# GpSimd makes more of the low weight parts in layer 1's mixer projections

## The chip, the cores and the metric

One core of a Trainium2 chip runs the whole kernel in one launch. The metric is the device time of one execution in microseconds. Five engines work from queues of their own, each strictly in the order in which the program puts instructions into it: TensorE (PE, with its weight loads as PEld), VectorE (DVE), ScalarE (ACT), GpSimd (POOL) and SyncE (SP), which here only starts transfers.

## The reference, cut to what matters

A two-layer decoder over 272 positions (16 meta tokens and 256 of the sequence), width 2048, float32. Each layer is a mixer and then a gated convolution FFN, with a residual around each. The change is in layer 1's mixer, whose first step is one large projection:

```
def mixer_cd(h, w_in, ...):
    z = h @ w_in                                  # 272 x 2048 by 2048 x 6416
    z_gla, z_rw = z[..., :GLA_COLS], z[..., GLA_COLS:]
    q, k, v, go, glr = jnp.split(z_gla, _splits(GLA_SIZES), axis=-1)
    ...
    o = gla_chunked(q, k, v, log_a)               # chunked gated linear attention
    ...
    r, kr, vr, xw, xa, xg = jnp.split(zr, _splits(RW_SIZES), axis=-1)
    ...
    y = rwkv7_scan(r, decay, kr, vr, kk, a)       # a recurrence over positions
    ...
    return jnp.concatenate([o, y], axis=-1) @ w_out
```

The kernel does the recurrence `rwkv7_scan` in chunks of 64 positions, for which it needs inverses of small triangular matrices: 128 of 32x32 and 16 of 16x16.

## The kernel before

Everything is a chain of weight multiplications of one form. A weight of 2048 rows by 128 columns is one projection; the mixer of layer 1 has 50 of them, called by `proj` in the order of the packed tensor `cd_in`. `gemm` and `gemm_steps` work a projection through in four parts of 512 columns of the packed weight (`SUB` = 4 tiles of 128x128). For precision each float32 weight part is split in two: ACT casts `wf` to a high part `wh` (L161), and another engine subtracts it again and leaves the low part `wl` (L163). Then PE runs three matmuls for each of the four tiles: high weight by high activation (L181), high by low (L182), low by high (L183). So a projection is 4 casts, 4 subtractions and 48 matmuls; its first matmul on the third low part is the 27th of them.

Who subtracts is decided by the argument `pool_lo`: the parts whose number (0 to 3) is in it go to GpSimd, the rest to VectorE:

```
eng = G if (k0 + s0) // SUB in pool_lo else V
lo = eng.tensor_sub(wl[:, :ns * P], src, wh[:, :ns * P].bitcast(F32))
```

`wh` and `wl` have five buffers each, so a part can be made at most five parts, one and a quarter projections, ahead of the matmuls that use it. Layer 0's mixer gives parts 0, 1 and 2 to GpSimd in most of its projections; layer 1's mixer gives it none.

The 50 projections of layer 1's mixer come in three blocks. The first ten (numbers 24, 25 and 8 to 15 of the recurrence's columns) bring the ranks, the gate and the keys. The next 24 are those of the gated linear attention, six for each of four heads; beside them runs the generator `prep`, which builds the recurrence's matrices (`stage_a`, `stage_b`, `stage_c` for eight head pairs) and inverts them. The last 16 bring the recurrence's `r` and `v`, and `rw_scan` runs beside them and beside the output projection.

The inversion is `lanes` (L645 to L665). It is GpSimd work from end to end: it fetches the matrices with a DMA issued on GpSimd's queue (L647), makes an identity (L649, L650), and does forward substitution, 31 steps of one multiplication (L656) and one addition (L658), each on the result of the step before, for the 32x32 matrices; the same with 15 steps for the 16x16 ones; a copy (L661); and DMAs to DRAM and back in another order (L662, L664, then L764, L767, L769), some of which wait on GpSimd's queue until an earlier one has landed. In the kernel before GpSimd has nothing else in its queue from the first step on until these are through.

The order in each engine's queue is not the order of the source: a scheduler in the framework sets it when the program is built, from its own estimate of durations, and it is fixed from then on.

Of the kernel before, what the change touches and what calls it, by code (L numbers as in the profile page):

```python
# [21 lines left out]
T = NM + SEQ  # L22
# [73 lines left out]
def _body(ctx, tc, nc, A):  # L96
# [47 lines left out]
    def tick():  # L144
        for t in list(side):
            try:
                next(t)
            except StopIteration:
                side.remove(t)
# [36 lines left out]
    def gemm(w, g, xs, n, pool_lo=()):  # L186
        acc = psA.tile([P, T], F32, tag="acc", name="acc")
        for _ in gemm_steps(w, g, xs, len(xs), acc[:, :n], pool_lo):
            tick()
        return acc[:, :n]  # L190
# [305 lines left out]
    def mixer_cd(tp, nm):  # L496
        xs = nm.xs()
        gi = [0]

        def proj(c0=0):  # L500
            gi[0] += 1
            return gemm(A["cd_in"], gi[0] - 1, [(a[:, c0:], b[:, c0:]) for a, b in xs], T - c0)

        def ring(name):
            return hpool.tile([P, T], F32, tag="h", name=name)
# [1 line left out]
        def shift(dst, i, c0=0, ps=None):  # L507
            if ps is None:
                ps = proj(c0)
            z = tp.tile([P, T + 16], F32, tag="z", name="z", bufs=2)  # L510
            V.tensor_mul(z[:, 1 + c0:T + 1], ps, nm.rstd[:, c0:])
            if c0:
                c0 += 1
                V.memset(dst[:, 0:c0], 0.0)
            else:
                V.memset(z[:, 0:1], 0.0)
            t = tp.tile([P, T], F32, tag="zt", name="zt", bufs=2)
            S.activation(t[:, c0:], z[:, 1 + c0:T + 1], AF.Copy, scale=omm[:, i:i + 1])
            V.scalar_tensor_tensor(dst[:, c0:], z[:, c0:T], pc("mu", i), t[:, c0:], op0=ALU.mult, op1=ALU.add)
# [22 lines left out]

        xt = ring("xt")
        ps24 = proj()
        nm.finish()
        glr = ring("glr")
        V.tensor_mul(glr, acc, nm.rstd)
        shift(xt, 24, 0, ps24)
        ps25 = proj(OUT - 2)
        logs, LD = [], []  # L550
        for q in range(4):
# [497 lines left out]
        c0, n = OUT, T - OUT  # L1049
# [146 lines left out]
```

## Time and profile before

| | |
|---|---|
| median of 3 runs | 2456.9 us (2455.43 to 2460.22) |
| the profiled execution | 2460.71 us, of which its span, first to last instruction, is 2458.9 us |
| PE busy | 2429.6 us, 99% of the span |
| DVE busy | 1792.7 us, 73% |
| ACT busy | 1338.1 us, 54% |
| POOL busy | 570.8 us, 23% |
| granted TensorE clock, mean | 0.998 |

Busy time counts an engine's instructions and not its waits, so a share is only an average over stages; which engine is late in a stage is read from that stage's windows and waits. Layer 1's mixer, up to its last scan, lies between about 1130 and 1640 us of the span.

### The profile page before, as it was taken

The page shows a single profiled execution, that of the slowest core. Times are in us where ns is not written, and L with a number is a line of the kernel's source. Part 1 is how long each engine was busy: PE and PEld are TensorE (multiplying, and loading weights), DVE is VectorE, ACT ScalarE, POOL GpSimd, SP SyncE. Part 2 cuts the span into 40 slices and gives each one's busy share as a digit, 9 for nine tenths or more (in the row PEclk, how much of TensorE's full clock was granted, in tenths as well). Part 3 has the DMA queues.
Part 4 walks back from the last instruction along what each step waited for, and adds up shares of the span by engine and source line. Part 5 has one row for each costly group of instructions (what it writes and reads, how often), then busy time and mean ns, then how long its engine had stood idle before and what let it go on. Part 6 is the DMA issues. An engine that isn't in the chain of part 4 may idle for free.

```text
span 2458.9 us, 53575 instructions
## 1 busy us (share of the span) xinstructions
PE 2429.6 (99%) x20476; PEld 2372.9 (97%) x20476; DVE 1792.7 (73%) x3400; ACT 1338.1 (54%) x2573; POOL 570.8 (23%) x894
## 2 busy tenths in 40 slices
PE   8999999999999999999999999999999999999998
PEld 8999999999999999999999988899999999999998
DVE  8897797777556677667786678879777755777754
ACT  5444655555445555546745445545656544656653
POOL 5677240000000000121148044416101000101122
PEclk9999999999999999999999999999999999999999
DMA  6555555555565555666445332345555566555564
GB/s 220 189 177 180 169 174 176 180 180 175 177 181 182 177 178 178 185 194 189 148 146 176 127 129 82 101 132 178 189 188 183 183 196 195 187 183 188 178 196 151
DMA packets 130991, 423.95 MB, mean 172 GB/s; under 512 B 18832, under 2 KB 27088, under 8 KB 130736
## 3 DMA queue, kind: packets, MB, share of 16 engines
q1 hardware_dynamic: 129104, 417.34, 53.0%
q8 instruction: 161, 2.64, 0.4%
q0 software_dynamic: 912, 2.55, 0.4%
q14 instruction: 94, 0.77, 0.1%
q10 hardware_dynamic: 720, 0.66, 0.1%
HBM read 414.41 MB, written 5.93 MB: 171 GB/s over the span
## 4 chain that ended last, share of the span: by engine, by line
PE 95%; DVE 2%; ACT 1%; DMA 1%; POOL 1%; issue 1%; SPq 0%; DVEq 0%; ACTq 0%; POOLq 0%
PE acc L181 24%; PE acc L183 23%; PE acc L182 23%; PE acc L176 7%; PE acc L175 7%; PE acc L174 6%; PE ps L932 1%; PE ps L966 1%; PE ps L947 0%; PE acc L178 0%; PE ps L981 0%; PE ps L834 0%; PE ps L989 0%; DVE wl L163 0%; DMA wf<-ab_in 0%
## 5 line engine op out<-in xcount | busy, mean ns | idle before, releaser
L161 ACT CAST wh<-wf 128x512 fp32r<-128x512 f32 (+1 forms) x1576 | 955.9, 611 | 876.8 <-PE acc L182 600.8
L163 DVE TENSOR_TENSOR wl<-wf,wh 128x512 fp32r<-128x512 f32 (+1 forms) x1465 | 1027.9, 707 | 463.7 <-ACT wh L161 418.8
L181 PE MATMUL acc<-x,wh 128*128 128x272 f32 (+2 forms) x2438 | 710.5, 291 | 1.3 <-ACT wh L161 1.3
L183 PE MATMUL acc<-x,wl 128*128 128x272 f32 (+2 forms) x2438 | 699.3, 287 | 1.0 <-DVE wl L163 1.0
L182 PE MATMUL acc<-x,wh 128*128 128x272 f32 (+2 forms) x2438 | 698.6, 287 | 0.0
L181 PEld LDWEIGHTS acc<-x,wh 128*128 128x128 f32 x2438 | 458.8, 188 | 15.4 <-issue 7.5
L183 PEld LDWEIGHTS acc<-x,wl 128*128 128x128 f32 x2438 | 458.9, 188 | 3.3 <-DVE wl L163 1.9
L182 PEld LDWEIGHTS acc<-x,wh 128*128 128x128 f32 x2438 | 459.6, 189 | 1.1 <-issue 0.3
L182 PE MATMUL acc<-act,wh 128*128 128x272 f32 (+1 forms) x1408 | 396.0, 281 | 0.0
L183 PE MATMUL acc<-act,wl 128*128 128x272 f32 (+1 forms) x1408 | 396.0, 281 | 0.0
L181 PE MATMUL acc<-act,wh 128*128 128x272 f32 (+1 forms) x1408 | 396.0, 281 | 0.0
L174 PE MATMUL acc<-x,wh 128*128 128x260 f32 x1144 | 323.6, 283 | 0.0
L176 PE MATMUL acc<-x,wl 128*128 128x258 f32 x1144 | 321.8, 281 | 0.0
L175 PE MATMUL acc<-x,wh 128*128 128x256 f32 x1144 | 321.0, 281 | 0.0
L181 PEld LDWEIGHTS acc<-act,wh 128*128 128x128 f32 x1408 | 264.8, 188 | 0.0
L182 PEld LDWEIGHTS acc<-act,wh 128*128 128x128 f32 x1408 | 264.7, 188 | 0.0
L183 PEld LDWEIGHTS acc<-act,wl 128*128 128x128 f32 x1408 | 264.7, 188 | 0.0
L175 PEld LDWEIGHTS acc<-x,wh 128*128 128x128 f32 x1144 | 215.6, 188 | 0.0
L174 PEld LDWEIGHTS acc<-x,wh 128*128 128x128 f32 x1144 | 215.5, 188 | 0.0
L176 PEld LDWEIGHTS acc<-x,wl 128*128 128x128 f32 x1144 | 215.3, 188 | 0.0
L163 POOL TENSOR_TENSOR wl<-wf,wh 128x512 fp32r<-128x512 f32 x111 | 148.1, 1342 | 57.3 <-ACT wh L161 54.9
L459 POOL MEMSET u<- 128x2 f32 x88 | 8.6, 100 | 573.3 <-DVE c L272 566.4
(341 smaller groups left out, 3743.9 us busy)
## 6 DMA issues: line engine op xcount, KB each, us to landing
wf<-up SPq DMA_DIRECT2D x352, 512.0 KB, 3.5
wf<-down SPq DMA_DIRECT2D x128, 512.0 KB, 3.8
wf<-cd_in SPq DMA_DIRECT2D x100, 512.0 KB, 3.6
wf<-ab_in SPq DMA_DIRECT2D x76, 512.0 KB, 3.6
wf<-down SPq DMA_DIRECT2D x64, 384.0 KB, 3.2
wf<-ab_out_s SPq DMA_DIRECT2D x16, 512.0 KB, 3.8
wf<-ab_out_a SPq DMA_DIRECT2D x16, 512.0 KB, 3.6
wf<-cd_out_o SPq DMA_DIRECT2D x16, 512.0 KB, 3.6
```

Source lines behind the costliest of these rows:

```text
L161: last_hi[0] = S.copy(wh[:, :ns * P], src)
L163: lo = eng.tensor_sub(wl[:, :ns * P], src, wh[:, :ns * P].bitcast(F32))
L174: PE.matmul(acc, a, x4, start=kk == 0, stop=False)
L175: PE.matmul(acc[:, 4:], a, x0, start=False, stop=False)
L176: PE.matmul(acc[:, 2:], b, x2, start=False, stop=False)
L181: PE.matmul(acc, a, xh, start=kk == 0, stop=False)
L182: PE.matmul(acc, a, xl, start=False, stop=False)
L183: PE.matmul(acc, b, xh, start=False, stop=kk == kt - 1)
L459: G.memset(u[:, 0:2], 0.0)
L932: PE.matmul(gv[:, :128], bkc, t[r, h0], start=True, stop=True)
L966: PE.matmul(wy[H[h0], 0:64], t[:, h0, 0:64], sv[:, h0], start=True, stop=True)
```

## The change

`proj` hands `gemm` a set of parts for GpSimd. In the first ten projections it is parts 1 and 3, so two of four; in the 40 after them it is part 2, one of four. That makes 20 + 40 = 60 subtractions of 128x512, moved from VectorE's queue to GpSimd's. Nothing is added or left out.

```diff
         def proj(c0=0):
             gi[0] += 1
-            return gemm(A["cd_in"], gi[0] - 1, [(a[:, c0:], b[:, c0:]) for a, b in xs], T - c0)
+            return gemm(A["cd_in"], gi[0] - 1, [(a[:, c0:], b[:, c0:]) for a, b in xs], T - c0,
+                        (1, 3) if gi[0] <= 10 else (2,))
```

The statement takes one line more than before, so every line below it has a number higher by one in the changed kernel: L656, L658 are L657, L659 there.

The scheduler places the moved subtractions in GpSimd's queue. In the orders below `wl` is a low part, `lanes` and `tm` are the inversion's matrix and its product. First the inversion of the 32x32 matrices, around its ninth and tenth step, before:

```order
L656 TENSOR_TENSOR tm<-lanes 128x192
L658 TENSOR_TENSOR lanes<-lanes,tm 128x24x8
L656 TENSOR_TENSOR tm<-lanes 128x207
L658 TENSOR_TENSOR lanes<-lanes,tm 128x23x9
L656 TENSOR_TENSOR tm<-lanes 128x220
L658 TENSOR_TENSOR lanes<-lanes,tm 128x22x10
```

The same queue now, at the three places in the inversion where a low part stands (rows between them are steps of the inversion alone):

```order
L659 TENSOR_TENSOR lanes<-lanes,tm 128x24x8
L657 TENSOR_TENSOR tm<-lanes 128x207
L163 TENSOR_TENSOR wl<-wf,wh 128x512
L659 TENSOR_TENSOR lanes<-lanes,tm 128x23x9
...
L659 TENSOR_TENSOR lanes<-lanes,tm 128x14x18
L163 TENSOR_TENSOR wl<-wf,wh 128x512
L657 TENSOR_TENSOR tm<-lanes 128x247
...
L657 TENSOR_TENSOR tm<-lanes 128x60
L163 TENSOR_TENSOR wl<-wf,wh 128x512
L659 TENSOR_TENSOR lanes<-lanes,tm 128x2x30
```

These are the third low parts of projections 20, 21 and 22, counted along PE's queue from the mixer's first. The one of projection 19 stands ahead of the first step, behind the DMA that fetches the matrices. Between that step and the part of projection 20 there are 17 multiplications and additions, then 19 up to the part of projection 21, then 23 up to the part of projection 22.

The second place is the end of the inversion, where GpSimd's queue holds DMAs. Before:

```order
L664 DMA scrN<-lanes 128x1024
L662 DMA scrT<-lanes 128x1024
L656 TENSOR_TENSOR tm<-lane_17689,lane_17688 16x28
L658 TENSOR_TENSOR lane_17689<-lane_17689,tm 16x14x2
L656 TENSOR_TENSOR tm<-lane_17689,lane_17688 16x39
L764 DMA tn<-scrN 32x32x32
L658 TENSOR_TENSOR lane_17689<-lane_17689,tm 16x13x3
L767 DMA lt<-scrT 32x32x32
```

Now:

```order
L657 TENSOR_TENSOR tm<-lane_17689,lane_17688 16x39
L765 DMA tn<-scrN 32x32x32
L163 TENSOR_TENSOR wl<-wf,wh 128x512
L659 TENSOR_TENSOR lane_17689<-lane_17689,tm 16x13x3
L768 DMA lt<-scrT 32x32x32
L657 TENSOR_TENSOR tm<-lane_17689,lane_17688 16x48
L768 DMA lt<-scrT 32x32x32
L659 TENSOR_TENSOR lane_17689<-lane_17689,tm 16x12x4
L765 DMA tn<-scrN 32x32x32
L163 TENSOR_TENSOR wl<-wf,wh 128x512
```

Here the low parts of projections 23 and 24 stand among the transfers that bring the inverses back; those of 25, 26 and 27 follow behind the rest of the transfers, behind the 16x16 steps and behind the last transfer. PE's own order of matmuls in these projections, the side work between them included, is the same before and now.

## Rows read from the trace of the kernel before

**Rows 1.** The page: busy time, share and instructions of each engine.
```profile
PE 2429.6 (99%) x20476; PEld 2372.9 (97%) x20476; DVE 1792.7 (73%) x3400; ACT 1338.1 (54%) x2573; POOL 570.8 (23%) x894
```

**Rows 2.** Windows of two stretches: length, busy PE, PEld, DVE, ACT, POOL, clock, DMA.
```profile
1280.00:1360.00 80.00, 80.00 (x615) 75.21 (x614) 55.53 (x95) 42.42 (x80) 62.07 (x104) 1.00 0.56 169
1420.00:1640.00 220.00, 218.04 (x2132) 184.28 (x2131) 182.48 (x509) 112.33 (x363) 84.29 (x173) 1.00 0.33 105
```

**Rows 3.** Waits of PE, 1130 to 1690: us in total, times, longest.
```profile
PE ps L728 <- DVE bk L716: 1.2, 2, 1.1
PE ps L932 <- POOL arc L922: 1.0, 2, 0.9
PE acc L183 <- DVE wl L163: 1.0, 3, 0.4
```

**Rows 4.** The page's groups of the subtraction: busy us, mean ns of one, idle before.
```profile
L163 DVE TENSOR_TENSOR wl<-wf,wh 128x512 fp32r<-128x512 f32 (+1 forms) x1465 | 1027.9, 707 | 463.7 <-ACT wh L161 418.8
...
L163 POOL TENSOR_TENSOR wl<-wf,wh 128x512 fp32r<-128x512 f32 x111 | 148.1, 1342 | 57.3 <-ACT wh L161 54.9
```

**Rows 5.** Timeline of POOL in the inversion: start us, us, instruction, idle before.
```profile
1276.05 0.51 POOL L647 DMA_DIRECT2D lane<-scr  x1
...
1276.60 0.31 POOL L649 MEMSET lane<- 16x256 f32 x1
...
1279.47 0.23 POOL L656 TENSOR_TENSOR tm<-lanes 128x31 f32<-128x31 f32 x1 [2.38 <-DMA lanes<-scr]
...
1291.54 1.08 POOL L658 TENSOR_TENSOR lanes<-lanes,tm 128x207 f32<-128x207 f32 x1
...
1308.67 0.60 POOL L656 TENSOR_TENSOR tm<-lanes 128x247 f32<-128x247 f32 x1
...
1325.27 0.36 POOL L658 TENSOR_TENSOR lanes<-lanes,tm 128x60 f32<-128x60 f32 x1
...
1337.24 0.80 POOL L767 DMA_DIRECT2D lt<-scrT  x1 [3.44 <-DMA scrT<-lanes]
...
1356.11 1.08 POOL L769 DMA_DIRECT2D lt<-scr0T  x2 [4.12 <-DMA scr0T<-lane]
```

**Rows 6.** Timeline of ACT: the cast for the third part of projection 19.
```profile
1278.82 0.62 ACT L161 CAST wh<-wf 128x512 fp32r<-128x512 f32 x1 [0.52 <-PE acc L182]
```

**Rows 7.** Timeline of PE: first matmul on the third low part, projections 20, 21, 22, 27.
```profile
1290.98 0.29 PE L183 MATMUL acc<-x,wl 128*128 128x272 f32 x1
...
1298.34 0.28 PE L183 MATMUL acc<-x,wl 128*128 128x258 f32 x1
...
1307.06 0.28 PE L183 MATMUL acc<-x,wl 128*128 128x258 f32 x1
...
1342.73 0.28 PE L183 MATMUL acc<-x,wl 128*128 128x258 f32 x1
```

**Rows 8.** Lines L656 and L658, 1291.6 to 1308.6: duration ns min/median/max.
```profile
L656 POOL TENSOR_TENSOR tm<-lanes x9: 566/622/961, 1292.7 to 1306.9; 128x252 f32<-128x252 f32 x2, 128x255 f32<-128x255 f32 x2, 128x220 f32<-128x220 f32 x1, 128x231 f32<-128x231 f32 x1
L658 POOL TENSOR_TENSOR lanes<-lanes,tm x10: 687/985/1214, 1291.5 to 1307.6; 128x252 f32<-128x252 f32 x2, 128x255 f32<-128x255 f32 x2, 128x207 f32<-128x207 f32 x1, 128x220 f32<-128x220 f32 x1
```

**Rows 9.** Timeline of PE at the start of the kernel: start us, us.
```profile
7.42 0.59 PE L181 MATMUL ps<-x,wh 128*128 128x272 f32 x1 [7.42 <-ACT wh L161]
...
13.10 0.43 PE L182 MATMUL ps<-x,wh 128*128 128x272 f32 x1
13.32 0.35 PE L183 MATMUL ps<-x,wl 128*128 128x272 f32 x1
```

**Rows 10.** Windows, the stretch after the last matmul: columns as in Rows 2.
```profile
2450.00:2455.00 5.00, 0.00 (x0) 0.00 (x0) 3.48 (x11) 0.00 (x0) 3.25 (x5) 0.56 0.80 281
```

**Rows 11.** Timeline of PE: first matmul on the fourth low part of projection 4.
```profile
1162.43 0.39 PE L183 MATMUL acc<-x,wl 128*128 128x272 f32 x1 [0.21 <-DVE wl L163]
```

**Rows 12.** Timelines in layer 0's mixer: subtractions of POOL and DVE that meet.
```profile
64.92 1.29 POOL L163 TENSOR_TENSOR wl<-wf,wh 128x512 fp32r<-128x512 f32 x1
...
65.01 1.75 DVE L163 TENSOR_TENSOR wl<-wf,wh 128x512 fp32r<-128x512 f32 x1
```

## The prediction

> **What bounds the kernel now.** I read the page's busy times first: PE is busy for 2429.6 of 2458.9 us [rows 1], so the kernel is one queue of matmuls, and an edit counts only by what it does to PE's waits. Next the windows of layer 1's mixer: PE 80.00 of 80 us in the stretch of the inversion, 218.04 of 220 in that of the scan, while DVE has 55.53 and 182.48 [rows 2]. So DVE, from which the change takes work, leaves PE little to wait for. PE's own waits in the mixer say the same: for DVE they come to 1.2 and 1.0 us, for POOL to 1.0 [rows 3]. The 2.2 us are about all that a quicker DVE can give back. Third I read GpSimd's timeline, since it gets the work: it is idle for most of the mixer, but in the inversion it is busy for 62.07 of 80 us [rows 2], in a row of steps that wait for each other. PE has no use for the inverses until much later, so that chain costs nothing today. It begins at 1279.47 and its last transfer is issued by 1357.19 (1356.11 + 1.08) [rows 5].
>
> **The change, part by part.** Moved are 60 subtractions. DVE loses 60 x 0.707 = 42 us of work; GpSimd gets 60 x 1.342 = 81 us [rows 4]. By sums both fit: they lie beside PE's work. But a low part that stands on GpSimd's queue behind the inversion's steps is made only when they are through, and PE, which takes its matmuls in order, waits for it. Nor can the other engines work around it: five buffers let them run one and a quarter projections ahead, and no further. So I set GpSimd's time between two such low parts, as the new order has them, against PE's time between their first uses. For each low part I add 1.4 us, the 1.34 of its mean [rows 4] and some 0.06 between two instructions.
>
> *Start.* The low part of projection 19 now stands ahead of the first step. Its cast ends at 1279.44 (1278.82 + 0.62) [rows 6], so it is done at about 1280.9; behind it come the second fetch and two small memsets, 0.9 us from 1276.05 to 1276.91 [rows 5]. First step: 1281.8 instead of 1279.47.
>
> *Projection 20.* 17 steps took 12.07 us (1279.47 to 1291.54) [rows 5]. 1281.8 + 12.1 + 1.4 = 1295.2, and PE wanted the part at 1290.98 [rows 7]. PE waits **4.2 us**.
>
> *Projection 21.* 19 steps took 17.13 us (1291.54 to 1308.67) [rows 5], with the low part 18.5. PE needs 1298.34 - 1290.98 = 7.36 us from the one use to the next [rows 7]. The wait would be 11.2 us. But these steps were not at their quickest: ten additions took between 687 and 1214 ns and nine multiplications between 566 and 961, of nearly equal sizes [rows 8]. What stretches them seems to be DVE's subtractions, which run beside them, and while PE waits DVE has little to do. If all were as short as the shortest it would be 10 x 0.687 + 9 x 0.566 + 19 gaps of 0.08 = 13.5 us, and the wait 7.5. DVE is active for about half of the interval, so I take the middle, 15.3: a wait of **9.3 us**.
>
> *Projection 22.* 23 steps took 16.60 us (1308.67 to 1325.27) [rows 5], with the low part 18.0; PE needs 8.72 us (1298.34 to 1307.06) [rows 7]. Wait 9.3; with all steps shortened in the ratio 13.5 : 17.1 it would be 5.8. Middle: **7.6 us**.
>
> *Projections 23 to 27.* From 1325.27 to 1357.19 is 31.9 us; five low parts add 7.0, of which 1.4 vanishes in the wait of 3.44 us for a transfer that is under way meanwhile [rows 5]: 37.5. PE needs 35.67 (1307.06 to 1342.73) [rows 7]. Alone that is 1.8. The clock comes on top: with no matmuls left the granted clock of the stretch is 0.56 on average [rows 10], that is for the most part the lower level, 1.2 GHz, and at the kernel's start matmuls stand 0.22 us apart until 13.5 us, though the first starts at 7.42 [rows 9]; the 48 of a projection at the full level have about 6 us, 0.125 each. So after a wait of 8 us or so some 6 us run at half speed and cost 3. Before the parts of projections 21 and 22 that is time which PE would wait anyway; after 22 it takes the place of the 1.8. I take **3.0 us** for this stretch.
>
> Sum in the inversion: 4.2 + 9.3 + 7.6 + 3.0 = 24.1 us. From projection 28 on GpSimd's queue is free again, and PE meets the inverses later in its order, as before.
>
> *Elsewhere.* In the first ten projections GpSimd has two parts, mostly with several us in hand. At one place PE already waits for the subtraction itself, at 1162.43 [rows 11]; GpSimd takes 1.342 - 0.707 = 0.6 us longer for it: **+0.6**. Where `stage_b` crowds DVE, the waits of 1.2 us and two of the three that make 1.0 [rows 3] should shrink: **-1.6**, between 0 and -2.2. In the scan stretch GpSimd gets 16 parts at 1.4, 22 us on top of 84.29 of 220 [rows 2]. What stands behind them feeds matmuls that come some 90 or more later in PE's order, over 9 us at the spacing above; I cost it at 0, between -2 (DVE's relief) and +2. DVE itself at 182.48 of 220 us [rows 2] loses 16 x 0.707 = 11 us and gains nothing that PE waits for.
>
> Together 24.1 + 0.6 - 1.6 = 23.1 us. Against the profiled execution, 2460.7 us with 1.8 outside its span, that is 2483.8; this one lay 3.8 above the median of the runs shown, so on 2456.9 I predict **2480.0 us**, 0.9% slower.
>
> Lower end: all steps at their shortest (the 17 steps too, 9.5 us, leave a wait of 1.7), no loss by the clock: 1.7 + 7.5 + 5.8 + 1.8 = 16.8, less 2.2 and 2: +12.6. Upper end: no step shortened, 4.2 + 11.2 + 9.3 + 3.0 = 27.7, with 0.6 and 2: +30.3.
>
> *A rule weighed against a row.* Where the two engines meet in layer 0's mixer, a subtraction of DVE that started at 65.01 beside one of POOL from 64.92 to 66.21 took 1.75 us [rows 12], 1.04 more than its mean of 0.707: it ended as if it had begun when POOL's was done. The Trainium skill, SBUF — State Buffer, section Who interferes with whom, says that a VectorE instruction with two SBUF inputs contends with a GpSimd instruction that reads SBUF, and that the second to issue blocks fully; the trace agrees in this pair. By it each part that is moved may cost DVE as much as it saves.
>
> **The rivals.**
> *The shared access makes DVE late (slower still).* If each of the 60 moved parts held a subtraction of DVE for 1.04 us, that is 62 us against 42 saved: 20 more. It decides only where DVE is as full as PE. Over the mixer's scan that is 16 x (1.04 - 0.71) = 5 us on 182.48 of 220, still free; for it speaks the crowd at `stage_b`. If all 20 reached PE: 2480 + 20 = 2500.
> *The scan's queue (slower still).* If the 16 parts each delayed the recurrence on GpSimd's queue by their 1.4 us and PE waited every time: +22, 2502. Against it: PE's waits for POOL there are 1.0 us in all [rows 3].
> *No change.* If the 19 steps before projection 21's part took no more than 5.9 us (7.36 less 1.4), the chain would be covered: 2457. Their shortest rows give 13.5.
> *Faster.* DVE's relief is worth more than its waits show. With PEld at 184.28 of 220 in the scan against 218.04 of PE [rows 2], PE's matmuls there are stretched by something; were that DVE's lateness, up to the 11 us taken from DVE could come back, and the 2.2 us [rows 3] with them. It decides from the point where the inversion costs less than 13 us, below the 16.8 of its shortest case: with 5 us of it left, 2449.
> That the change isn't made as meant is no case: the new order shows the parts on GpSimd.
>
> **How the numbers follow.** 0.2% of the time is 4.9 us, about what a measurement of this kernel can tell from no change. The inversion's queue as worked out: 0.84. DVE made late 0.05, the scan's queue 0.05, no change 0.03, faster 0.03. Slower by over 0.2%: 0.84 + 0.05 + 0.05 = 0.94; same 0.03; faster 0.03. The range takes the ends of the likeliest case, 2469.5 and 2487.2, and some of the two slower rivals on top: 2469 to 2490.
>
> **What would show it.** Right: PE is idle before L183 in projections 20, 21 and 22, released by POOL's `wl` L163, some 4, 9 and 8 us, within about 1280 to 1335; POOL's steps stay in one row, with single low parts between them; all that follows is about 23 us later; the granted clock has one or two dips there. POOL's busy time is some 80 us higher, DVE's some 40 lower. Wrong: no such waits, or PE's waits spread over the scan with POOL's `arc` or `sp` as releaser, or DVE's subtractions beside POOL's at 1.5 us and more with PE waiting for those.

## The result, and the profile after

The changed kernel took 2485.6 us at the median of three runs (2482.2 to 2488.6) against 2456.9: 1.011 times, 95% interval 1.0096 to 1.0124. Four more runs later in the study gave a median of 2482.9 against 2457.5, 1.0101 (1.0087 to 1.0115). So it is slower by 25 to 29 us; 2480.0 was predicted.

The page, its busy times and the two groups of the subtraction, answers to [rows 1, 4]:

```profile
PE 2435.4 (98%) x20476; PEld 2379.4 (96%) x20476; DVE 1768.6 (71%) x3340; ACT 1338.2 (54%) x2573; POOL 644.9 (26%) x954
...
L163 DVE TENSOR_TENSOR wl<-wf,wh 128x512 fp32r<-128x512 f32 (+1 forms) x1405 | 988.6, 708 | 483.4 <-ACT wh L161 441.6
...
L163 POOL TENSOR_TENSOR wl<-wf,wh 128x512 fp32r<-128x512 f32 x171 | 231.4, 1359 | 196.3 <-ACT wh L161 142.9
```

The 60 parts moved at about the price forecast: DVE's subtractions fell by 39.3 us, GpSimd's rose by 83.3. But DVE's whole busy time fell by 24.1 only: its other instructions became longer, by 12 us when their times in the two traces are added up one by one, by 15 as the difference of the busy times.

PE's longest waits in layer 1's mixer (us in total, times, longest), which answer to [rows 3]:

```profile
PE acc L183 <- POOL wl L163: 17.4, 6, 6.5
PE ps L729 <- DVE bk L717: 3.1, 7, 1.0
PE acc L181 <- ACT wh L161: 1.9, 1, 1.9
```

GpSimd's low parts are the new first row, 17.4 us from nothing. The two rows that were to shrink did two different things: the waits for DVE's `wl` are no longer in the list, those for its `bk` went from 1.2 to 3.1.

To say where the time went I set the same matmuls of both kernels against each other. PE's timeline of the kernel before, the first matmul on the first low part of projections 1, 6, 20, 28, and of a later one behind the scan:

```profile
1135.94 0.29 PE L183 MATMUL acc<-x,wl 128*128 128x272 f32 x1
...
1173.73 0.29 PE L183 MATMUL acc<-x,wl 128*128 128x272 f32 x1
...
1287.99 0.29 PE L183 MATMUL acc<-x,wl 128*128 128x272 f32 x1
...
1346.90 0.28 PE L183 MATMUL acc<-x,wl 128*128 128x258 f32 x1
...
1658.27 0.29 PE L183 MATMUL acc<-ysp,wl 128*128 128x258 f32 x1
```

The same five in the timeline of after, with the six waits for GpSimd's parts (idle time and releaser in brackets; the last of them is at projection 37) and the one for a cast ahead of the first:

```profile
1132.31 0.29 PE L183 MATMUL acc<-x,wl 128*128 128x272 f32 x1
...
1158.74 0.39 PE L181 MATMUL acc<-x,wh 128*128 128x272 f32 x1 [1.94 <-ACT wh L161]
...
1160.14 0.59 PE L183 MATMUL acc<-x,wl 128*128 128x272 f32 x1 [0.88 <-POOL wl L163]
...
1172.05 0.28 PE L183 MATMUL acc<-x,wl 128*128 128x272 f32 x1
...
1288.71 0.29 PE L183 MATMUL acc<-x,wl 128*128 128x272 f32 x1
...
1295.13 0.39 PE L183 MATMUL acc<-x,wl 128*128 128x272 f32 x1 [3.25 <-POOL wl L163]
...
1310.83 0.58 PE L183 MATMUL acc<-x,wl 128*128 128x258 f32 x1 [6.54 <-POOL wl L163]
...
1326.69 0.39 PE L183 MATMUL acc<-x,wl 128*128 128x258 f32 x1 [2.66 <-POOL wl L163]
...
1358.80 0.39 PE L183 MATMUL acc<-x,wl 128*128 128x272 f32 x1 [2.10 <-POOL wl L163]
...
1370.48 0.28 PE L183 MATMUL acc<-x,wl 128*128 128x258 f32 x1
...
1451.62 0.39 PE L183 MATMUL acc<-x,wl 128*128 128x260 f32 x1 [2.00 <-POOL wl L163]
...
1679.95 0.29 PE L183 MATMUL acc<-ysp,wl 128*128 128x258 f32 x1
```

Read the distances, not the times: projection 1 comes 3.6 us earlier after, in code that is the same in both; that is about what the profiled execution of before lay above its median. From 1 to 6 it was 37.79 us and is 39.74 (+1.95). From 6 to 20: 114.26, now 116.66 (+2.40). From 20 to 28, the inversion: 58.91, now 81.77 (+22.86). From 28 to the end of the scan: 311.37, now 309.47 (-1.90). Together +25.3. The profiled execution of after is the fastest of its three; the 3.4 us by which their median lies above it are in no trace.

Inside the inversion the waiting matmuls carry on from [rows 7]: to the third part of 20, 2.99 became 6.42 (+3.43); from there to that of 21, 7.36 became 15.70 (+8.34); to that of 22, 8.72 became 15.86 (+7.14); and from there to projection 28, 39.84 became 43.79 (+3.95).

The windows of after (columns as in [rows 2]) show what the waits do to the clock:

```profile
1160.00:1165.00 5.00, 4.86 (x23) 4.16 (x24) 4.95 (x7) 3.96 (x8) 3.62 (x4) 0.66 0.63 208
...
1290.00:1300.00 10.00, 6.75 (x42) 6.52 (x42) 2.51 (x5) 2.48 (x4) 9.14 (x14) 0.83 0.29 106
1300.00:1310.00 10.00, 4.30 (x31) 3.32 (x29) 2.03 (x4) 1.60 (x3) 9.06 (x14) 0.84 0.00 0
1310.00:1320.00 10.00, 9.17 (x41) 8.90 (x42) 2.23 (x4) 3.69 (x7) 9.06 (x14) 0.50 0.34 107
1320.00:1330.00 10.00, 7.34 (x39) 6.20 (x39) 2.99 (x6) 1.93 (x4) 9.14 (x18) 0.84 0.24 81
```

Between 1310 and 1320 PE is busy for 9.17 us and starts 41 matmuls, where before it started 77 in ten (615 in the 80 of [rows 2]): the granted clock is 0.50, the lower level. POOL is busy for 9 of every 10 us, DVE for 2 to 3.

GpSimd's timeline of after: the parts of projections 19, 20, 21, 22 and 26, the steps right behind them, and one step between (start us, us):

```profile
1280.25 1.85 POOL L163 TENSOR_TENSOR wl<-wf,wh 128x512 fp32r<-128x512 f32 x1 [3.52 <-ACT wh L161]
...
1282.92 0.31 POOL L657 TENSOR_TENSOR tm<-lanes 128x31 f32<-128x31 f32 x1
...
1293.81 1.26 POOL L163 TENSOR_TENSOR wl<-wf,wh 128x512 fp32r<-128x512 f32 x1
1295.03 0.59 POOL L659 TENSOR_TENSOR lanes<-lanes,tm 128x207 f32<-128x207 f32 x1
...
1297.72 0.96 POOL L659 TENSOR_TENSOR lanes<-lanes,tm 128x231 f32<-128x231 f32 x1
...
1309.52 1.26 POOL L163 TENSOR_TENSOR wl<-wf,wh 128x512 fp32r<-128x512 f32 x1
1310.74 0.60 POOL L657 TENSOR_TENSOR tm<-lanes 128x247 f32<-128x247 f32 x1
...
1325.38 1.26 POOL L163 TENSOR_TENSOR wl<-wf,wh 128x512 fp32r<-128x512 f32 x1
...
1357.50 1.25 POOL L163 TENSOR_TENSOR wl<-wf,wh 128x512 fp32r<-128x512 f32 x1
```

Each of the last four follows GpSimd's own row without idle time and ends within 0.1 us of the start of the matmul that waits for it: 1293.81 + 1.26 is 1295.07, PE starts at 1295.13.

### The profile page after: what moved, and what is told of

It reads as the page before. It is cut to its first block, busy times and chain, and to the rows that moved or that the text cites. A ratio compares the mean times of both kernels' runs of the same rounds, so it can differ in the third digit from the quotient of the medians.

```text
span 2480.4 us, 53634 instructions
## 1 busy us (share of the span) xinstructions
PE 2435.4 (98%) x20476; PEld 2379.4 (96%) x20476; DVE 1768.6 (71%) x3340; ACT 1338.2 (54%) x2573; POOL 644.9 (26%) x954
## 4 chain that ended last, share of the span: by engine, by line
PE 93%; POOL 3%; DVE 2%; issue 1%; DMA 1%; ACT 1%; SPq 0%; DVEq 0%; POOLq 0%; ACTq 0%
PE acc L181 23%; PE acc L182 22%; PE acc L183 22%; PE acc L176 7%; PE acc L175 7%; PE acc L174 6%; POOL tm L657 1%; POOL lanes L659 1%; PE ps L933 1%; PE ps L967 1%; POOL wl L163 0%; PE ps L948 0%; PE acc L178 0%; PE ps L982 0%; PE ps L990 0%
## 5 line engine op out<-in xcount | busy, mean ns | idle before, releaser
L163 DVE TENSOR_TENSOR wl<-wf,wh 128x512 fp32r<-128x512 f32 (+1 forms) x1405 | 988.6, 708 | 483.4 <-ACT wh L161 441.6
L183 PE MATMUL acc<-x,wl 128*128 128x272 f32 (+2 forms) x2438 | 702.1, 288 | 17.4 <-POOL wl L163 17.4
L181 PEld LDWEIGHTS acc<-x,wh 128*128 128x128 f32 x2438 | 461.8, 189 | 16.1 <-issue 7.6
L163 POOL TENSOR_TENSOR wl<-wf,wh 128x512 fp32r<-128x512 f32 x171 | 231.4, 1359 | 196.3 <-ACT wh L161 142.9
```

What stands on the lines that cost most here:

```text
L181: PE.matmul(acc, a, xh, start=kk == 0, stop=False)
L183: PE.matmul(acc, b, xh, start=False, stop=kk == kt - 1)
```

## The experiments

Most of them change the expression that picks GpSimd's parts and nothing else in the source. The scheduler then orders the queues anew, and PE's order of matmuls, as the traces have it, need not stay as in before. From projection 16 to 35 it is the same in all the kernels whose edit is in that expression alone. Between 12 and 15 it differs where parts of 11 to 18 are moved; behind that stretch it differs from projection 36 on where the parts from 28 or 29 on are moved, and from 41 on where only those from 39 on are.

**Where the loss lies: four shares of the change.** Projections 19 to 27 taken back; these alone; the first ten alone; 28 and later alone.

```diff
-                        (1, 3) if gi[0] <= 10 else (2,))
+                        (1, 3) if gi[0] <= 10 else () if 19 <= gi[0] <= 27 else (2,))
+                        (2,) if 19 <= gi[0] <= 27 else ())
+                        (1, 3) if gi[0] <= 10 else ())
+                        (2,) if gi[0] >= 28 else ())
```

> Only the third parts of projections 19 to 27 are moved, nine subtractions. Theory (inversion's queue): nearly the whole loss is here; in the trace of after the stretch cost 22.9 us, so 2480 us (2477 to 2483), with PE waits for GpSimd's wl of about 3.3, 6.5, 2.7 and 2.1 us in projections 20, 21, 22 and 26. Rival (shared access): 9/60 of the loss, 2461. Rival (scan's queue): 2457.

Measured: 2480.8 against 2456.6, 1.0096 (1.0081 to 1.0112), +24.2. Nine of the 60 subtractions carry the loss. PE's four waits came to 15.1 us, the places as in after; from projection 20 to 28 it lost 25.6 us, and its order of matmuls is that of before through the whole mixer.

> Theory (the inversion's queue on GpSimd): the 51 parts of projections 1 to 18 and 28 to 50 cost little, the loss sits in the nine parts of 19 to 27 that are taken back here. In the trace of after, PE lost 4.3 us between projections 1 and 20 and won 2 back behind 28; so 2459 us (2457 to 2462). Rival (shared access makes DVE late everywhere): 51 of 60 parts still moved, so 51/60 of the 28.7 us stay, 2481. Rival (scan's queue): the 16 parts of the recurrence still moved, 2479 to 2485.

Measured: 2468.8 (2461.4 to 2470.3), 1.004 (1.0028 to 1.0053), +12.2: the shared-access and scan rivals are both too high, but so much was not expected of my own theory either. The profiled execution was the fastest of the five. In it 4.8 us were lost up to projection 20 and 1.7 at projection 28, where PE waited for GpSimd's part. The 9 us that other runs took on top are in no trace; the kernel from 28 on shows where they can lie.

> Only the 20 parts of the first ten projections are moved. Theory: these cost about 1.9 us, at projection 4, where PE waited 1.94 us for a cast and 0.88 us for the part and the clock fell; 2459 us (2456 to 2461). Rival (shared access makes DVE late, 20 of 60 parts): 2466. Rival (DVE's relief shows): 2455 or less.

Measured: 2459.7, 1.0012 (1.0003 to 1.0021), +3.1. Its trace repeats after's loss at projection 4 (+1.96 from 1 to 6) and nothing until 20.

> Only the third parts of projections 28 to 50 are moved, 23 of them, 16 in the recurrence. Theory: they lie beside PE's work; the trace of after won 2 us back behind projection 28, so 2455 us (2454 to 2458). Rival (scan's queue): 16 x 1.4 = 22 us, 2479. Rival (shared access): 23/60 of the loss, 2468.

Measured: 2463.9 (2459.0 to 2467.9), 1.003 (1.0019 to 1.0041), +7.3. Wrong, and the theory has a hole there. PE's timeline at projection 28's third part in this kernel:

```profile
1352.88 0.58 PE L183 MATMUL acc<-x,wl 128*128 128x258 f32 x1 [5.84 <-POOL wl L163]
```

and GpSimd's ahead of it:

```profile
1350.46 1.08 POOL L770 DMA_DIRECT2D lt<-scr0T  x2 [1.45 <-DMA scr0T<-lane]
1351.54 2.50 POOL L163 TENSOR_TENSOR wl<-wf,wh 128x512 fp32r<-128x512 f32 x2
```

The inversion's tail is still on GpSimd's queue: projection 28's part stands behind the last fetch, which waits for a transfer. Up to projection 29 this cost 9.9 us; from there to the end of the scan 1.9 came back, as in after. In after itself PE is so late at 28 that the tail is through.

**The place of that hole.** 28 is left out too, and then all up to 38.

```diff
-                        (1, 3) if gi[0] <= 10 else (2,))
+                        (2,) if gi[0] >= 29 else ())
+                        (2,) if gi[0] >= 39 else ())
```

> Only the third parts of projections 29 to 50 are moved: projection 28, whose part waited 5.8 us behind the tail of the inversion, is taken back. Theory: the scan's stretch gives 1.9 us, as in the traces of after, of the kernel without the inversion's parts and of the one from 28 on; 2454.7 us (2453.5 to 2456.5), 1 or 2 us better than before. Rival (scan's queue on GpSimd): what that last kernel lost was in the scan, and it stays: 2462 or more.

Measured: 2455.2 against 2457.2, 0.9992 (0.9983 to 1.0001), -1.9. One subtraction, that of projection 28, makes the difference between +7.3 and this. The scan's queue is no rival any more, except at one place: in projection 37 PE waited 2.0 us for a part that stood behind a row of copies of `arc` and two products `bp`. There the scheduler's new order shows too: the product that in before waited for `arc` in projection 36 stands later in PE's queue and waits no more. PE won 2.2 us by the first part of projection 37, and lost 4.0 between there and projection 40.

> Only the third parts of projections 39 to 50 are moved, twelve of the sixteen of the recurrence. In the trace of the kernel from 29 on, PE lost 1.9 us between projections 36 and 40 (a wait of 2.0 us for GpSimd's part of projection 37) and won 2.4 back between 40 and 54. Theory (parts cost where they queue behind GpSimd's own row, and give a little where they don't): without the first, 2.4 us better than before, 2455.0 (2454 to 2456). Rival (what is won behind 40 is only the time lost ahead of it): 2457.4, as before.

Measured: 2454.9 against 2457.3, 0.9989 (0.998 to 0.9998), -2.4: a version faster than both kernels, by little. In its trace 0.5 us are won between projections 40 and 50 and 1.7 between 50 and the end of the scan, a stretch in which PE's waits in before come to 0.1 us. Whether DVE's relief gave these 2.2 us or the other order of PE's matmuls is not shown.

**One subtraction, and what the clock adds.** Only projection 21's part is moved; then the same, with 75 matmuls into a spare bank ahead of the one that waits.

```diff
-                        (1, 3) if gi[0] <= 10 else (2,))
+                        (2,) if gi[0] == 21 else ())
...
+    def spare(n, d, a, x): [PE.matmul(d, a, x, start=True, stop=True) for _ in range(n)]
...
-                    PE.matmul(acc, a, xl, start=False, stop=False)
+                    PE.matmul(acc, a, xl, start=False, stop=False); fill and eng is G and k == 0 and spare(fill, psb()[:, :256], a, xh[:, :256])
...
+                        (2,) if gi[0] == 21 else (), fill=75 if gi[0] == 21 else 0)
```

> One subtraction of all is moved: the third part of projection 21. Theory (in-order queue): 37 steps of the inversion stand ahead of it, which before were through at about 1309 us where PE wanted the part at 1298.3; less 1.5 us that the steps win while DVE is quiet: one PE wait of 10 us, and 3.5 us more at half clock behind it (what projection 21 lost so in the trace of after), so 2470 us (2467 to 2473). Rival (the loss is a sum of many small delays that the moved parts share): 1/60 of 28.7, 2457.

Measured: 2472.3 against 2457.2, 1.006 (1.0046 to 1.0074), +15.1. PE and the windows there:

```profile
1307.40 0.58 PE L183 MATMUL acc<-x,wl 128*128 128x258 f32 x1 [12.13 <-POOL wl L163]
```

```profile
1300.00:1305.00 5.00, 0.00 (x0) 0.00 (x0) 0.00 (x0) 0.00 (x0) 4.45 (x8) 0.50 0.00 0
...
1310.00:1315.00 5.00, 5.00 (x23) 4.96 (x24) 2.08 (x4) 1.93 (x6) 4.45 (x8) 0.50 0.72 253
```

A wait of 12.1 us, 12.3 of delay at this matmul, and 3.9 more up to projection 23, at half clock. One moved subtraction costs over half of what sixty do; the loss is no sum of small delays.

> As the kernel with only projection 21's part moved, and PE runs 75 matmuls of 256 columns that no result uses, some 9 us, right before the matmul that waits. If the loss behind the wait is the clock that fell in it: the granted clock stays at 1.00 there and 3.5 us of that kernel's loss vanish, 2467 us. Rival (what is lost behind the wait is casts and parts that come late): no gain, 2470.

Measured: 2470.0, 1.0055 (1.0039 to 1.007), +12.8. PE's timeline, then the same windows:

```profile
1295.29 9.15 PE L142 MATMUL ps<-x,wh 128*128 128x256 f32 x75
...
1306.67 0.39 PE L183 MATMUL acc<-x,wl 128*128 128x258 f32 x1 [2.23 <-POOL wl L163]
```

```profile
1300.00:1305.00 5.00, 4.43 (x37) 4.23 (x36) 0.00 (x0) 0.00 (x0) 4.45 (x8) 1.00 0.00 0
...
1310.00:1315.00 5.00, 5.00 (x36) 4.20 (x34) 3.25 (x6) 3.66 (x6) 4.53 (x7) 1.00 0.51 202
```

The matmul on the part is delayed by 11.4 us in place of 12.3, little less, but the clock stays at 1.00, 36 matmuls start where 23 did, and behind the wait 0.1 us is lost up to projection 22's third part in place of 3.9. PE then waited 0.7 us for DVE at another place (the state `gst` of the linear attention). The medians lie 2.3 us apart, the profiled executions 3.8; with these spreads the time alone does not tell the theory from its rival, whose 2470 was met only because the kernel it was set against took 2472.3. The trace does: that the useless matmuls kept the clock is shown. The Trainium skill, TensorE: Matmul & The Clock Gate, section What's actually happening, says that it is activity that releases the throttle; these two traces agree.

**What stretches GpSimd's steps.** As with projections 19 to 27 alone, but without DVE's own subtractions there.

```diff
-                wl = wpool.tile([P, SUB * P], F32R, tag="wl", name="wl")
-                lo = eng.tensor_sub(wl[:, :ns * P], src, wh[:, :ns * P].bitcast(F32))
+                wl = wh if bare and eng is V else wpool.tile([P, SUB * P], F32R, tag="wl", name="wl")
+                lo = None if wl is wh else eng.tensor_sub(wl[:, :ns * P], src, wh[:, :ns * P].bitcast(F32))
...
-                        (1, 3) if gi[0] <= 10 else (2,))
+                        (2,) if 19 <= gi[0] <= 27 else (), bare=19 <= gi[0] <= 27)
```

> As the kernel with only the parts of projections 19 to 27 moved, but DVE's subtractions of these nine projections are left out (PE multiplies the high part a second time in place of the low one). Theory (DVE's subtractions stretch GpSimd's steps): the steps keep to their shortest, the 17, 19 and 17 steps up to the parts of 20, 21 and 22 take 9.5, 13.0 and 13.7 us in place of 10.9, 14.5 and 14.6, and the loss shrinks by 3.8 us: 2477 us (2475 to 2478.5). Rival (the steps' spread has another source): 2481 as with the subtractions.

Measured: 2473.3 against 2457.2, 1.0064 (1.0051 to 1.0078), +16.1. GpSimd's timeline of this kernel:

```profile
1277.68 0.33 POOL L657 TENSOR_TENSOR tm<-lanes 128x31 f32<-128x31 f32 x1
...
1286.52 1.27 POOL L163 TENSOR_TENSOR wl<-wf,wh 128x512 fp32r<-128x512 f32 x1
1287.76 0.60 POOL L659 TENSOR_TENSOR lanes<-lanes,tm 128x207 f32<-128x207 f32 x1
...
1290.45 0.64 POOL L659 TENSOR_TENSOR lanes<-lanes,tm 128x231 f32<-128x231 f32 x1
...
1301.27 1.26 POOL L163 TENSOR_TENSOR wl<-wf,wh 128x512 fp32r<-128x512 f32 x1
```

Seventeen steps take 8.84 us (10.89 in after), the nineteen behind them 13.51 (14.49), and the addition of 128x231 takes 0.64 where after's took 0.96. Beside that one stood this row of DVE in after:

```profile
1297.26 0.93 DVE L163 TENSOR_TENSOR wl<-wf,wh 128x512 fp32r<-128x512 f32 x1 [5.68 <-ACT wh L161]
```

The stretch is DVE's, as supposed. The whole gain, 8 us, is twice the 3.8 forecast, which makes the forecast a miss. In the trace 4.4 us of it lie at the three stretches that it was worked out from. The rest comes mostly from the small inverses, which shrink too: the part of projection 26 now costs PE next to nothing where it had cost about 4 with its half clock.

**The stretch of `stage_b`.** The eight parts of projections 11 to 18 alone.

```diff
-                        (1, 3) if gi[0] <= 10 else (2,))
+                        (2,) if 11 <= gi[0] <= 18 else ())
```

> Only the third parts of projections 11 to 18 are moved, eight subtractions, none in the inversion or the scan. Theory after the traces: GpSimd's parts lie beside the bk products of both engines there, PE's waits for bk grow, and it costs the 2.4 us that after lost between projections 12 and 15: 2459.5 us (2458 to 2461). Rival (the prediction's own term, DVE's relief at stage_b): 1.6 us faster, 2455.5.

Measured: 2459.2 against 2457.5, 1.0006 (0.9997 to 1.0015), +1.7, too little for the time alone to settle. The trace does: PE's waits for `bk` are 3.1 us in 7 as in after, and the loss from projection 6 to 20 is 2.4 as there. Some relief came: the two waits of before for DVE's own low parts in projection 14, 0.8 us together, are gone. The waits for `bk` outweigh it. DVE's products `bk` between 1215 and 1265 of before, and then of after (duration ns min/median/max):

```profile
L716 DVE TENSOR_TENSOR bk<-kn,pi x16: 475/489/1152, 1222.6 to 1262.5; 64x320 f32<-64x320 f32 x16
```

```profile
L717 DVE TENSOR_TENSOR bk<-kn,pi x16: 474/689/1453, 1221.0 to 1263.4; 64x320 f32<-64x320 f32 x16
```

The first two of them in after, 1.97 us for what two medians of before make 0.98, stand beside this part of GpSimd's, twice as long as alone:

```profile
1219.97 2.61 POOL L163 TENSOR_TENSOR wl<-wf,wh 128x512 fp32r<-128x512 f32 x1 [3.60 <-ACT wh L161]
```

The moved parts take more from DVE than they give. Added up from the traces between the first matmuls of projections 11 and 19, DVE's 24 subtractions take 18.0 us where its 30 took 22.6, but its other 104 instructions take 51.9 where they took 46.0. PE's and DVE's orders differ from before here too; but the two places where PE waits longest, 1.3 and 1.0 us in two waits each, stand within one matmul of where they stood in its queue, and there it had not waited. The Trainium skill, SBUF — State Buffer, section Who interferes with whom, has just this pair (two SBUF inputs on DVE against a GpSimd instruction that reads SBUF); the rows agree.

**The spread of after's runs.** The changed kernel again, and beside it one without the parts of projections 27 and 28.

```diff
-                        (1, 3) if gi[0] <= 10 else (2,))
+                        (1, 3) if gi[0] <= 10 else () if gi[0] in (27, 28) else (2,))
```

> The changed kernel once more, beside the next one. Its runs lay between 2482.2 and 2488.6 us, and the profiled one was the lowest of them. Theory: the spread comes from GpSimd's wait for the transfer of the small inverses, which stands ahead of the parts of projections 27 and 28: runs from 2482 to 2489 again, median 2484 to 2486. Rival (the spread was of that chip): 2482 to 2483.

> As the changed kernel, but the third parts of projections 27 and 28, the two that stand behind the transfer of the small inverses, are left on DVE. Theory: without them nothing waits behind that transfer, the runs keep together at the profiled time of after, 2482 us (2480.5 to 2483.5), and the median is 2 to 3 us below that of the changed kernel. Rival (the spread is elsewhere): the same median and spread as the changed kernel.

Measured: 2482.9 (2481.5 to 2484.2) and 2483.7 (2482.8 to 2484.8). The two are the same, and the theory of the last transfer falls: in after PE is late enough that neither part is waited for. The trace of the changed kernel repeated the first one's delays against before within 0.2 us all through the mixer. What the slowest of the first three runs did, 2488.6, stays open.

## Why the prediction held, step by step

*The queue.* Right, with its places, its releaser and its sizes. Start of the first step: 1281.8 was forecast; it came at 1282.92, of which 0.7 is the kernel's delay up to there and the rest due to a part that took 1.85 us in place of 1.34. Then **4.2**, **9.3**, **7.6** and **3.0** us were forecast for projections 20, 21, 22 and 23 to 27, 24.1 in all; measured 3.4, 8.3, 7.1 and 4.0, 22.9 in all. These are delays: PE's idle time at the three parts was 3.3, 6.5 and 2.7 us, not the "4, 9 and 8" named as the sign, because most of the rest of the second and the third delay is PE running at half clock on its way to the part.

*The steps' length.* The middle between the rows of before and the shortest was right in kind and a little long: 15.3 with the part 16.7, measured 14.49 and 15.7. That DVE's subtractions stretch the steps was a guess in the prediction; the kernel without them shows it. I left the first 17 steps unshortened, 12.1; they took 10.89.

*The clock.* Right: the lower level behind the waits of projections 20, 21 and 22. Ahead of projections 21 and 22 it vanished in the next wait, as argued. The 3.0 for projections 23 to 27 measured 3.95: 1.7 behind 22 by the clock, and 2.3 by the one wait of projection 26, whose part stood behind a row of the small inverses' steps; the parts of 23, 24, 25 and 27 were not waited for.

*Elsewhere.* Here the sum was wrong: -1.0 forecast, +2.45 measured. Projection 4: +0.6 forecast, +1.95 measured; the wait for a cast grew from 1.28 to 1.94 us, that for the part from 0.21 [rows 11] to 0.88, and the clock, which had stayed at 1.00 there, fell to 0.66. Before:

```profile
1161.70 0.39 PE L181 MATMUL acc<-x,wh 128*128 128x272 f32 x1 [1.28 <-ACT wh L161]
```

```profile
1160.00:1165.00 5.00, 3.51 (x22) 2.50 (x21) 3.95 (x9) 4.33 (x10) 0.64 (x2) 1.00 0.42 129
```

The part's own length came out, 0.67 us for the 0.6; the step that failed is that a slower part costs its own length only. How much more it costs is uncertain: the kernels that move nothing in the first ten projections lost between 0 and 1.14 us from projection 1 to 6 against the trace of before, those that move the first ten's parts between 1.95 and 3.07. `stage_b`: **-1.6** forecast, +2.4 measured. The waits for DVE's own low parts did go, 0.8 us; what failed is that "the waits of 1.2 us" for `bk` should shrink: I took work from DVE there and did not ask what GpSimd does at the same time on the same access, though the row weighed in the prediction showed it. Scan: 0 forecast, -1.9 measured, within the -2 to +2 given for it. That the whole came out so near is in part luck: the inversion, 1.2 us too high, and the scan, 1.9 too high, made up for most of the 5.4 by which the other two terms were too low.

*One statement was wrong without a cost.* "From projection 28 on GpSimd's queue is free again": the kernel with the parts from 28 on waits 5.84 us at 28 for it. In the change the inversion's own delay covers that.

*The rivals.* Shared access was real, most of the 2.4 us at `stage_b` and not 20. The scan's queue showed at projection 37 alone, 2.0 us. The 2.2 us of PE's waits for DVE were counted too low: the same view of before has 0.7 us more for `sv` and 0.5 for `xd`. Of the 13 us that could come back by the faster rival, the parts from 39 on give 2.4, and that it is DVE's relief that gives them is not shown. That more buffers would have hidden the queue was not tried.

## What to carry to other kernels

An engine's idle share did not tell here what a piece of work put on its queue would cost; what counted is the longest chain that stood ahead of it there, against the time until somebody needed it. One subtraction behind such a chain cost 15 us here, and twelve at places without one gained 2.4. Ask of every wait on TensorE's path what the clock does behind it, and of every instruction given to GpSimd what DVE reads beside it.

## What the runs showed of the hardware that was not expected

A GpSimd subtraction of 128x512 takes 1.26 us beside a quiet DVE, 1.85 or 2.61 beside a busy one; a DVE product of 64x320 between 0.47 and 1.45 in the same way. A wait of 2.1 us at projection 26 was followed by a lower granted clock in one kernel (0.69 between 1355 and 1360, with the parts of 19 to 27 alone) and not in another (1.00 between 1350 and 1365 in after). At projection 4 the clock fell to 0.77 between 1160 and 1165 even where nothing is moved there (projection 21's part alone), and stood at 1.00 in before. So the price of a short wait differs by 1 or 2 us from one kernel to the next; what decides it stays open.
